# Sevenfold products of a SwiGLU layer in one sequence for every row pair, an earlier place for the first piece of the next matrix, and held-back opening loads

## The chip, the cores and the metric

The kernel runs on one core of a Trainium2 chip (trn2). The metric is device microseconds of one execution. A core has TensorE (PE, matmuls), VectorE (DVE), ScalarE (ACT), GpSimd (POOL) and SyncE (SP); each runs its own instructions in the order of the program, and they wait for one another by semaphores. DMAs are issued here by SP and by POOL.

## The reference

A decoder trunk of two layers on x (1 x 256 x 2048, float32): 256 tokens, width 2048.

```python
def swiglu(x, w_in, w_out):
    g, u = jnp.split(x @ w_in, 2, axis=-1)
    return (jax.nn.silu(g) * u) @ w_out

for layer in range(DEPTH):                      # DEPTH = 2
    hn = rms_norm(h, norm_mix[layer])
    mix = mlstm_mixer(...) if layer % N_MIXERS == 0 else rglru_mixer(...)
    h = h + mix
    h = h + swiglu(rms_norm(h, norm_ffn[layer]), ffn_w_in[layer], ffn_w_out[layer])
return rms_norm(h, norm_final)
```

The change touches only swiglu: w_in is 2048 x 11264 (2 x 5632), w_out 5632 x 2048.

## The kernel before, in words

**Number format.** Every float32 matrix is split into a high part (whi, whix, whit, whio: casts on ACT, L266 and L930) and a low part (wlo, wlox, wlot, wloo: subtractions on DVE, L267). One product is three matmuls: L829, L830 and L831; in most of them L830 reads the low part of the weights.

**The first matrix** (`inner`, `pairs`). It is worked off in 11 blocks j of 512 columns of gate and of 512 of up, each block in 8 row pairs p of 256 rows. A "plain" pair (p=0 always, more in block 0) is eight products into four PSUM banks P2, Q5, Q3 and P4. The other pairs are done by seven products in Strassen's manner, P1, P2, Q3, Q5, P7, Q6 and P4, in the order of the table PRODUCTS; they add up in seven banks over the pairs of the block. P1, P2 and Q3 read whix and wlox (the loaded rows), the other four read whit and wlot (sums of rows, made on DVE at L310, L313 and L314 and split at L266 and L267). Pair 7, the last, has an order of its own, LAST: P1, Q6, P7, Q5, P2, Q3, P4.

**The end of a block.** ds is a buffer with four slices, s0, d0, d1, s1 (`ds`). ACT copies P1 into s0 (L865); DVE makes d0 = Q6 - s0 (L866), d1 = d0 - P7 (L868), adds Q5 to s1 and d0's slices (L871), adds P2 to s0 (L874), Q3 to d0 (L876), takes d1 from P4 (L877); ACT applies silu to s0 (L875) and to d1 (L878); two products on DVE (L880) finish it. PE then transposes the result (tv, L889), and ACT casts it (hh, L543).

**The second matrix** (`outs`, `piece`). The block's 512 rows of w_out are done in 8 pieces: quarters q = 0..3 of the columns by b = 0, 1 (token halves), twelve matmuls each, named out with j, q and b: out420 is block 4, q=2, b=0. Block j's pieces q=0 and 1 are placed in pairs 4 to 7 of block j+1, q=2 and 3 in pairs 0 to 3 of block j+2. The function `between` places them: it is called after every product with left = minus the number of products still to come in the pair, and puts the next piece at left = -2 (even pairs) or -3 (odd pairs). A piece opens by an ACT copy of the sum so far into its bank (L949) and ends by an ACT copy back (L960).

**The load of the second matrix.** Per quarter there are two halves of 256 rows. Half i=0: SP loads rawo, ACT casts whio (L266), DVE subtracts (L267). Half i=1: POOL loads rawo (L923); ACT writes wloo = -rawo (L928); POOL issues a DMA that adds the same weights onto wloo (L929); ACT casts whio (L930). What then stands in wloo is the low part, made without DVE. These names carry j, q and i: wloo421 is block 4, q=2, i=1. It is read by the last six of a piece's twelve matmuls, first by the eighth.

**The order.** Each engine's order is fixed when the program is built, by a scheduler with priorities (`tc.high_priority`), so an edit in one place can move instructions of other engines. "Opening" means block 0 of a layer, where the normalised activations (c_f, L474; p_f) are still being made, raw0_5 is the load of pair 5, and the first two rawo loads of w_out are issued ahead of need.

Of the kernel before, what the change touches and what calls it, by code (L numbers as in the profile page):

```python
# [11 lines left out]
ALU = mybir.AluOpType  # L12
# [23 lines left out]
    ("P1", "A11", "B11"), ("P2", "A12", "B21"), ("Q3", "A3", "B22"),  # L36
    ("Q5", "A5", "T1"), ("P7", "A7", "T3"), ("Q6", "A6", "T2"), ("P4", "A22", "T4"),
)

LAST = tuple(sorted(PRODUCTS, key=lambda c: ("P1", "Q6", "P7", "Q5", "P2", "Q3", "P4").index(c[0])))  # L40
SEVEN = ("A12", "A22", "A11", "A5", "A7", "A6", "A3")


# [1 line left out]
def kernel(  # L45
# [21 lines left out]
    nc = tc.nc  # L67
# [209 lines left out]
    def stream4(w, c0, nk):  # L277

        wv = w.rearrange("(k p) n -> p k n", p=P)
        for kg in range(0, nk, 4):  # L280
# [5 lines left out]
            for i in range(4):  # L286
                yield kg + i, *both[i]

    def is_plain(j, p):
        return p not in SEVENS or j == 0 and p in BOTH  # L290

    def pairs(w, j, held):

        wv = w.rearrange("(k p) n -> p k n", p=P)
        for p in range(NK // 2):
            raw = four("raw", f"{j}_{p}", F32, 3)
            if held and j == 0 and p == 0:

                nc.vector.tensor_copy(raw[0:1, 0, 0:1], h[0:1, NT - 1, 2 * NB - 1:2 * NB])
            for i, c0 in enumerate((j * NB, FF + j * NB)):  # L300
                nc.sync.dma_start(raw[:, 2 * i:2 * i + 2, :], wv[:, 2 * p:2 * p + 2, c0:c0 + NB])
            if is_plain(j, p):
                with tc.high_priority(offset=AHEAD):
                    both = halves(f"{j}_{p}", raw)
                yield p, both
                continue

            with tc.high_priority(offset=AHEAD):
                t = four("sum", f"{j}_{p}", F32, 1)
                nc.vector.tensor_tensor(  # L310
                    t[:, 0:2, :], raw[:, 1:3, :], raw[:, 3:4, :].broadcast_to([P, 2, NB]), op=ALU.add
                )
                nc.vector.tensor_tensor(t[:, 2, :], t[:, 0, :], raw[:, 2, :], op=ALU.add)  # L313
                nc.vector.tensor_tensor(t[:, 3, :], t[:, 2, :], raw[:, 0, :], op=ALU.add)  # L314
                both = halves(f"x{j}_{p}", raw, 3) + halves(f"t{j}_{p}", t, step=2)
            yield p, dict(zip(("B21", "B11", "B22", "T1", "T3", "T2", "T4"), both))
# [489 lines left out]
    NP = NK // 2  # L806

    def ffn(layer, n, nxt):
# [24 lines left out]
        def inner(j, between):  # L833

            ps = {}

            def add(c, a, b, stop):
                first = c not in ps
                if first:
                    ps[c] = bank(c, f"{c}_{j}")  # L840
                product(ps[c], a, b, first, stop)


            ds = fp.tile([P, 4, NB], F32, tag="ds", name=f"ds{j}")
            d0, d1, s0, s1 = (ds[:, i, :] for i in range(4))
            last = max(p for p in SEVENS if not is_plain(j, p))
            for p, ops in pairs(w, j, layer == 1):
                if is_plain(j, p):

                    work = [  # L850
                        (c, n.plain(p, f)[a], ops[2 * side + f], p == NP - 1 and f == 1)
                        for c, side, a in (("Q5", 1, 1), ("P2", 0, 0), ("Q3", 1, 2), ("P4", 0, 1)) for f in range(2)
                    ]
                else:
                    seven = n.seven(p)
                    work = [
                        (c, seven[a], ops[b], p == (last if c in ("P7", "P1", "Q6") else NP - 1))
                        for c, a, b in (LAST if p == NP - 1 else PRODUCTS)
                    ]
                for i, job in enumerate(work):  # L860
                    add(*job)
                    between(j, p, i + 1 - len(work))
                if p == last:
                    with tc.high_priority(offset=AHEAD):
                        nc.scalar.copy(s0, ps["P1"])  # L865
                        nc.vector.tensor_tensor(d0, ps["Q6"], s0, op=ALU.subtract)  # L866

                        nc.vector.tensor_tensor(d1, d0, ps["P7"], op=ALU.subtract)  # L868
            with tc.high_priority(offset=AHEAD):

                nc.vector.tensor_tensor(  # L871
                    ds[:, 0:4:3, :], ps["Q5"].unsqueeze(1).broadcast_to([P, 2, NB]), ds[:, 0:2, :], op=ALU.add
                )
                nc.vector.tensor_tensor(s0, ps["P2"], s0, op=ALU.add)  # L874
                nc.scalar.activation(s0, s0, AF.Silu, scale=n.rstd[:, 0:1])  # L875
                nc.vector.tensor_tensor(d0, ps["Q3"], d0, op=ALU.add)  # L876
                nc.vector.tensor_tensor(d1, ps["P4"], d1, op=ALU.subtract)  # L877
                nc.scalar.activation(d1, d1, AF.Silu, scale=n.rstd[:, 1:2])  # L878
                for b, (u, g) in enumerate(((d0, s0), (s1, d1))):
                    nc.vector.scalar_tensor_tensor(  # L880
                        out=u, in0=u, scalar=n.rstd[:, b:b + 1], in1=g, op0=ALU.mult, op1=ALU.mult
                    )
            return d0, s1
# [13 lines left out]
        def outs(j, hi, lo):  # L897

            wv = ffn_w_out[layer][j * NB:(j + 1) * NB, :].rearrange("(k p) n -> p k n", p=P)
            held = {}

            def load(q, last):
                held.clear() if not last else None
                tiles = held[q] = []
                if last:
                    raw = four("raw", f"o{j}{q}", F32, 2)
                    for i in (0, 2):  # L910
                        nc.sync.dma_start(raw[:, i:i + 2, :], wv[:, i:i + 2, q * NB:(q + 1) * NB])
                    with tc.high_priority(offset=AHEAD):
                        tiles.extend(halves(f"o{j}{q}", raw))
                    return
                for i in range(2):

                    spare = "1" if i and q % 2 else ""
                    raw, wh, wl = (
                        pool_of(f"{what}o{at}").tile([P, 2, NB], dt, tag=f"{what}{i}", name=f"{what}o{j}{q}{i}")
                        for what, dt, at in (("raw", F32, ""), ("whi", F32R, ""), ("wlo", F32R, spare))  # L920
                    )
                    src = wv[:, 2 * i:2 * i + 2, q * NB:(q + 1) * NB]
                    (nc.gpsimd if i else nc.sync).dma_start(raw, src)  # L923
                    with tc.high_priority(offset=AHEAD):
                        if i:

                            with after(*copies[-2:-1]):
                                nc.scalar.activation(wl, raw, AF.Copy, scale=-1.0)  # L928
                            nc.gpsimd.dma_start(wl, src, accum_op=ALU.add)  # L929
                            nc.scalar.copy(wh, raw)  # L930
                        else:
                            split(wh, wl, raw)
                    tiles.extend((wh[:, k, :], wl[:, k, :]) for k in range(2))

            def piece(q, b, last=False):
                if b == 0:
                    load(q, last)
                tiles = held[q]
                bs = slice(b * P, (b + 1) * P)
                hs = h[:, b, q * NB:(q + 1) * NB]  # L940
                name = f"out{j}{q}{b}"
                o = acc(name) if last else pool_of("out").tile([P, NB], F32, tag="out", name=name)


                ends = q == 3 and last and nxt.lag and j == NJ - 1
                first = False if ends else last or fresh.pop() if last or fresh else False
                if not first:
                    with tc.high_priority(offset=AHEAD):
                        nc.scalar.copy(o, hs)  # L949
                for k in range(4):  # L950
                    product(o, (hi[:, k, bs], lo[:, k, bs]), tiles[k], first and k == 0, k == 3, skip_group_check=True)
                if ends:

                    nxt.store(b, o)
                    return
                with tc.high_priority(offset=AHEAD):
                    if first:
                        nc.vector.tensor_tensor(hs, o, hs, op=ALU.add)
                    else:
                        copies.append(nc.scalar.copy(hs, o))  # L960

            return [(piece, q, b) for q in range(4) for b in range(NT)]

        work, turns, late = [], [], []

        def between(j, p, left):

            if left == -2 - p % 2 and work:
                piece, *at = work.pop(0)
                piece(*at)  # L970
            if left == 0 and p == 0:
# [258 lines left out]
```

## Time and profile before

| | us |
|---|---|
| median of 3 runs | 2096.39 (2095.75 to 2098.28) |
| the profiled execution | 2094.86 |
| its span in the trace | 2093.1 |
| mean granted PE clock | 0.998 |
| the two swiglu stretches | about 397 to 1083 and 1390 to 2093 |

The profile lists, by engine, when each instruction started and how long it took; busy shares add these up. In a timeline a row reads: start in us, duration in us, engine, line, operation, output and inputs, and in brackets the time that the engine had been idle and what ended it. Matmuls are pipelined: a row of 0.39 us is followed by the next 0.23 us later. A row with x8 is eight instructions in one.

### The profile page before, as it was taken

How to read it: one execution, taken by the hardware profiler on the slowest of the kernel's cores; microseconds unless marked ns; L12 is line 12 of the kernel's file. 1: busy time of each engine (PE TensorE's matmuls, PEld its weight loads, DVE VectorE, ACT ScalarE, POOL GpSimd, SP SyncE). 2: the span in 40 equal slices, each digit the busy share in tenths (PEclk: the TensorE clock that was granted, in tenths of full speed). 3: DMA queues.
4: the chain of work that ended last, by engine and by line, in shares of the span. 5: the costliest groups of instructions: out<-in, count | busy, mean ns of one | idle time of the engine just before them, and what ended most of it. 6: DMA issues, size and time to landing. Idle time of an engine off the chain costs nothing.

```text
span 2093.1 us, 27909 instructions
## 1 busy us (share of the span) xinstructions
PE 2068.5 (99%) x10424; PEld 1738.0 (83%) x10424; DVE 1746.0 (83%) x1930; ACT 1429.0 (68%) x1739; POOL 195.9 (9%) x218
## 2 busy tenths in 40 slices
PE   9999999999999999999999999999999999999998
PEld 8988888877888888888879999887788888888886
DVE  6655556699999999999976787669999999999995
ACT  5444455567777777877864778556787777887775
POOL 0011110000111111111100000000011111111112
PEclk9999999999999999999999999999999999999999
DMA  7556667656878878888765666665787888888784
GB/s 229 170 162 180 181 177 225 187 178 202 254 223 251 234 223 250 241 237 237 224 197 155 191 190 187 219 214 175 218 243 231 242 232 240 242 228 245 231 238 153
DMA packets 223135, 446.66 MB, mean 213 GB/s; under 512 B 16328, under 2 KB 17048, under 8 KB 222872
## 3 DMA queue, kind: packets, MB, share of 16 engines
q1 hardware_dynamic: 189832, 362.02, 53.5%
q0 software_dynamic: 32448, 81.80, 18.1%
q8 instruction: 81, 1.33, 0.3%
q10 hardware_dynamic: 720, 1.07, 0.1%
q14 instruction: 54, 0.44, 0.1%
HBM read 442.74 MB, written 2.10 MB: 213 GB/s over the span
## 4 chain that ended last, share of the span: by engine, by line
PE 73%; DVE 11%; issue 6%; ACT 4%; DMA 4%; POOL 1%; SPq 0%; ACTq 0%; POOLq 0%; DVEq 0%
PE out L829 5%; PE out L830 5%; PE out L831 5%; PE P L830 5%; PE P L831 5%; PE P L829 5%; PE Q L829 4%; PE Q L830 4%; PE Q L831 4%; DMA rawo<-in_ffn_w_out_dram 3%; DVE wlot L267 2%; DVE wlox L267 2%; PE po L328 2%; PE po L327 2%; PE po L326 2%
## 5 line engine op out<-in xcount | busy, mean ns | idle before, releaser
L266 ACT CAST whit<-sum 128x1024 fp32r<-128x1024 f32 x288 | 301.3, 1050 | 182.4 <-DVE sum L310 144.2
L242 DVE TENSOR_TENSOR wlo<-raw,whi 128x1024 fp32r<-128x1024 f32 (+1 forms) x226 | 273.5, 1213 | 172.3 <-ACT whi L241 169.8
L267 DVE TENSOR_TENSOR wlot<-sum,whit 128x1024 fp32r<-128x1024 f32 x288 | 348.9, 1221 | 36.0 <-ACT whit L266 34.6
L241 ACT CAST whi<-raw 128x1024 fp32r<-128x1024 f32 (+1 forms) x226 | 234.5, 1042 | 193.6 <-PE po L328 40.4
L829 PE MATMUL out<-whio,hh 128*128 128x512 f32 x704 | 275.5, 392 | 1.0 <-ACT hh L543 0.5
L830 PE MATMUL out<-wloo,hh 128*128 128x512 f32 x704 | 273.9, 390 | 0.0
L831 PE MATMUL out<-whio,hh 128*128 128x512 f32 x704 | 273.6, 390 | 0.0
L267 DVE TENSOR_TENSOR wlox<-raw,whix 128x1536 fp32r<-128x1536 f32 x144 | 252.5, 1753 | 23.4 <-ACT whix L266 23.0
L266 ACT CAST whix<-raw 128x1536 fp32r<-128x1536 f32 x144 | 213.6, 1483 | 25.4 <-PE P L831 24.2
L310 DVE TENSOR_TENSOR sum<-raw 128x1024 f32<-128x1024 f32 x144 | 176.2, 1223 | 3.9
L929 POOL DMA_DIRECT2D wloo<-in_ffn_w_out_dram x78 | 94.0, 1205 | 702.9 <-ACT wloo L928 678.2
L829 PEld LDWEIGHTS out<-whio,hh 128*128 128x128 f32 x704 | 132.2, 188 | 30.7 <-ACT out L949 1.7
L830 PEld LDWEIGHTS out<-wloo,hh 128*128 128x128 f32 x704 | 132.2, 188 | 28.2 <-DVE wloo L267 0.7
L831 PEld LDWEIGHTS out<-whio,hh 128*128 128x128 f32 x704 | 132.1, 188 | 27.8
L960 ACT COPY h<-out 128x512 f32<-128x512 f32 x154 | 89.8, 583 | 65.3 <-PE out L831 65.2
L923 POOL DMA_DIRECT2D rawo<-in_ffn_w_out_dram x78 | 59.1, 758 | 755.3 <-ACT whio L930 362.6
L267 DVE TENSOR_TENSOR wloo<-rawo,whio 128x1024 fp32r<-128x1024 f32 (+1 forms) x88 | 117.9, 1339 | 4.4 <-ACT whio L266 4.4
L829 PE MATMUL Q<-whit,p_f 128*128 128x512 f32 x288 | 113.9, 400 | 5.2 <-ACT whit L266 4.5
L830 PE MATMUL P<-wlox,p_f 128*128 128x512 f32 x288 | 113.3, 393 | 4.0 <-DVE wlox L267 3.8
L829 PE MATMUL P<-whix,p_f 128*128 128x512 f32 x288 | 112.3, 398 | 2.7 <-ACT whix L266 2.7
L830 PE MATMUL P<-wlot,p_f 128*128 128x512 f32 x288 | 112.6, 391 | 1.7 <-DVE wlot L267 1.7
L830 PE MATMUL Q<-wlot,p_f 128*128 128x512 f32 x288 | 113.2, 397 | 0.1
(296 smaller groups left out, 5240.9 us busy)
## 6 DMA issues: line engine op xcount, KB each, us to landing
raw<-in_ffn_w_in_dram SPq DMA_DIRECT2D x352, 512.0 KB, 4.8
rawo<-in_ffn_w_out_dram SPq DMA_DIRECT2D x98, 512.0 KB, 6.0
raw<-in_m_w_in_dram SPq DMA_DIRECT2D x94, 512.0 KB, 3.8
rawo<-in_ffn_w_out_dram POOLq DMA_DIRECT2D x78, 512.0 KB, 5.9
wloo<-in_ffn_w_out_dram POOLq DMA_DIRECT2D x78, 512.0 KB, 6.4
raw<-in_r_w_in_dram SPq DMA_DIRECT2D x64, 512.0 KB, 3.9
raw<-in_m_w_out_dram SPq DMA_DIRECT2D x32, 512.0 KB, 3.7
raw<-in_r_w_out_dram SPq DMA_DIRECT2D x32, 512.0 KB, 4.2
```

Of the source, the lines that this page charges most:

```text
L241: nc.scalar.copy(hi[:, i:i + step, 0:ncols], r)
L242: nc.vector.tensor_tensor(lo[:, i:i + step, 0:ncols], r, hi[:, i:i + step, 0:ncols].bitcast(F32), op=ALU.subtract)
L266: nc.scalar.copy(hi, src)
L267: nc.vector.tensor_tensor(lo, src, hi.bitcast(F32), op=ALU.subtract)
L310: nc.vector.tensor_tensor(t[:, 0:2, :], raw[:, 1:3, :], raw[:, 3:4, :].broadcast_to([P, 2, NB]), op=ALU.add)
L326: nc.tensor.matmul(o, lhsT=ah[:, bs], rhs=hi, start=(k == 0), stop=False)
L829: nc.tensor.matmul(o, lhsT=a[0], rhs=b[0], start=start, stop=False, **kw)
L830: nc.tensor.matmul(o, lhsT=a[0], rhs=b[1], start=False, stop=False, **kw)
L831: nc.tensor.matmul(o, lhsT=a[1], rhs=b[0], start=False, stop=stop, **kw)
L923: (nc.gpsimd if i else nc.sync).dma_start(raw, src)
L929: nc.gpsimd.dma_start(wl, src, accum_op=ALU.add)
L960: copies.append(nc.scalar.copy(hs, o))
```

## The change

It has five parts.

1. LAST is gone: pair 7 takes the order of PRODUCTS like all others.
2. A plain pair's products come in the order P2, Q5, Q3, P4 instead of Q5, P2, Q3, P4.
3. Where the last sevenfold pair is p=7 (blocks 1 to 10), P1 is copied by ACT twice, into s0 and into d0 (one more ACT copy per block); P2 is added to s0 early, ahead of Q6; Q6 is taken with d0.
4. In pair 0 `between` puts the piece at left = -6, after the two P2 products, instead of at -2, after six.
5. In block 0, for q=0, the two rawo buffers are first written, one element each, by a POOL copy from raw0_5 (`seen`), so that the loads into them can't start before raw0_5 has landed.

```diff
-LAST = tuple(sorted(PRODUCTS, key=lambda c: ("P1", "Q6", "P7", "Q5", "P2", "Q3", "P4").index(c[0])))
...
+    seen = []
...
+            if j == 0 and p == 5:
+                seen.append(raw)
...
-                        for c, side, a in (("Q5", 1, 1), ("P2", 0, 0), ("Q3", 1, 2), ("P4", 0, 1)) for f in range(2)
+                        for c, side, a in (("P2", 0, 0), ("Q5", 1, 1), ("Q3", 1, 2), ("P4", 0, 1)) for f in range(2)
...
-                        for c, a, b in (LAST if p == NP - 1 else PRODUCTS)
+                        for c, a, b in PRODUCTS
...
                         nc.scalar.copy(s0, ps["P1"])
-                        nc.vector.tensor_tensor(d0, ps["Q6"], s0, op=ALU.subtract)
+                        first = s0
+                        if p == NP - 1:
+                            first = d0
+                            nc.scalar.copy(d0, ps["P1"])
+                            nc.vector.tensor_tensor(s0, ps["P2"], s0, op=ALU.add)
+                        nc.vector.tensor_tensor(d0, ps["Q6"], first, op=ALU.subtract)
...
-                nc.vector.tensor_tensor(s0, ps["P2"], s0, op=ALU.add)
+                if last < NP - 1:
+                    nc.vector.tensor_tensor(s0, ps["P2"], s0, op=ALU.add)
...
+                    if j == 0 and q == 0:
+                        nc.gpsimd.tensor_copy(raw[0:1, 0, 0:1], seen[-1][0:1, 0, 0:1])
                     (nc.gpsimd if i else nc.sync).dma_start(raw, src)
...
-            if left == -2 - p % 2 and work:
+            if left == (-2 - p % 2 if p else -6) and work:
```

In the changed kernel line numbers shift: L829 to L831 become L831 to L833, L865 becomes L867 (and L872 is the new copy), L875 and L878 become L884 and L887, L923, L928, L929 and L930 become L935, L940, L941 and L942, L949 and L960 become L961 and L972, L266 becomes L264, L889 becomes L898, L543 becomes L545.

What the scheduler makes of it, at three places of layer 1. First PE at the start of block 6, before, from the third row of Q3 of pair 0 to the first matmul that reads wloo421 (names: bank, block; weights, block and pair; activation):

```order
8621 L830 MATMUL Q3_6_15340<-wlo6_0_15323,p0_f1_11986 128x512
8622 L831 MATMUL Q3_6_15340<-whi6_0_15322,p0_f1_11986 128x512
8623 L829 MATMUL Q3_6_15340<-whi6_0_15322,p0_f1_11986 128x512
8624 L830 MATMUL Q3_6_15340<-wlo6_0_15323,p0_f1_11986 128x512
8625 L831 MATMUL Q3_6_15340<-whi6_0_15322,p0_f1_11986 128x512
8626 L830 MATMUL out420_15360<-wloo420_15349,hh4_14814 128x512
8627 L831 MATMUL out420_15360<-whio420_15348,hh4_14814 128x512
8628 L829 MATMUL out420_15360<-whio420_15348,hh4_14814 128x512
8629 L830 MATMUL out420_15360<-wloo420_15349,hh4_14814 128x512
8630 L831 MATMUL out420_15360<-whio420_15348,hh4_14814 128x512
8631 L829 MATMUL out420_15360<-whio421_15354,hh4_14814 128x512
8632 L830 MATMUL out420_15360<-wloo421_15355,hh4_14814 128x512
```

The same piece in the changed kernel, from the third row of P2 of pair 0:

```order
8630 L833 MATMUL P2_6_15345<-whi6_0_15341,p0_f1_11998 128x512
8631 L831 MATMUL P2_6_15345<-whi6_0_15341,p0_f1_11998 128x512
8632 L832 MATMUL P2_6_15345<-wlo6_0_15342,p0_f1_11998 128x512
8633 L833 MATMUL P2_6_15345<-whi6_0_15341,p0_f1_11998 128x512
8634 L831 MATMUL out420_15365<-whio420_15353,hh4_14832 128x512
8635 L832 MATMUL out420_15365<-wloo420_15354,hh4_14832 128x512
8636 L833 MATMUL out420_15365<-whio420_15353,hh4_14832 128x512
8637 L831 MATMUL out420_15365<-whio420_15353,hh4_14832 128x512
8638 L832 MATMUL out420_15365<-wloo420_15354,hh4_14832 128x512
8639 L833 MATMUL out420_15365<-whio420_15353,hh4_14832 128x512
8640 L831 MATMUL out420_15365<-whio421_15359,hh4_14832 128x512
8641 L832 MATMUL out420_15365<-wloo421_15360,hh4_14832 128x512
```

The piece out420 moved from behind P2, Q5 and Q3 of pair 0 to behind P2; Q5, Q3 and P4 now follow it. In pair 7 ahead of it stand P1, P2, Q3 and Q5, the piece out411, then P7, Q6 and P4 (before: P1, P7, Q6 and Q5, then out411, then P2, Q3 and P4).

Second ACT at the same boundary, before: from the copy of P1 to the silu of s0.

```order
1299 L865 COPY ds5_14815<-P1_5_14910 128x512
1300 L266 CAST whi6_0_15322<-raw6_0_15319 128x2048
1301 L928 ACTIVATE wloo421_15355<-rawo421_15353 128x1024
1302 L266 CAST whio420_15348<-rawo420_15347 128x1024
1303 L960 COPY h_73<-out411_15282 128x512
1304 L930 CAST whio421_15354<-rawo421_15353 128x1024
1305 L949 COPY out420_15360<-h_73 128x512
1306 L875 ACTIVATE ds5_14815<-ds5_14815,rstd_f1_12669 128x512
```

In the changed kernel, from the copies of P1 to the copy into out420:

```order
1302 L867 COPY ds5_14833<-P1_5_14928 128x512
1303 L872 COPY ds5_14833<-P1_5_14928 128x512
1304 L264 CAST whi6_0_15341<-raw6_0_15338 128x2048
1305 L884 ACTIVATE ds5_14833<-ds5_14833,rstd_f1_12681 128x512
1306 L264 CAST whio420_15353<-rawo420_15352 128x1024
1307 L940 ACTIVATE wloo421_15360<-rawo421_15358 128x1024
1308 L972 COPY h_73<-out411_15300 128x512
1309 L942 CAST whio421_15359<-rawo421_15358 128x1024
1310 L961 COPY out420_15365<-h_73 128x512
```

The L928 that writes wloo421 (now L940) stood directly behind whi6_0; between them stand now the silu and the cast whio420, and ahead of whi6_0 there is one copy more. It is so at pair 7 of blocks 3, 5, 7 and 9 in both layers, and at that of block 2 the L960 copy stands ahead of it too. At pair 7 of blocks 4, 6 and 8 the L928 of q=2 keeps its place between the two casts of whit of pair 7.

Third ACT in the boundary after that, block 6 to block 7, before: the silu of d1 among the casts of pair 1. The last row writes wloo531.

```order
1362 L266 CAST whix7_1_15906<-raw7_1_15899 128x1536
1363 L266 CAST whit7_1_15910<-sum7_1_15902 128x1024
1364 L878 ACTIVATE ds6_15318<-ds6_15318,rstd_f1_12669 128x512
1365 L266 CAST whit7_1_15910<-sum7_1_15902 128x1024
1366 L960 COPY h_73<-out520_15863 128x512
1367 L928 ACTIVATE wloo531_15995<-rawo531_15993 128x1024
```

In the changed kernel:

```order
1366 L264 CAST whix7_1_15926<-raw7_1_15919 128x1536
1367 L264 CAST whit7_1_15930<-sum7_1_15922 128x1024 x2
1368 L972 COPY h_73<-out520_15869 128x512
1369 L940 ACTIVATE wloo531_16015<-rawo531_16013 128x1024
1370 L961 COPY out521_15949<-h_73 128x512
1371 L887 ACTIVATE ds6_15337<-ds6_15337,rstd_f1_12681 128x512
```

The silu of d1 (L878, now L887) stood ahead of the L928 that writes wloo531; it now stands behind it and behind the copy into out521. It is so at the end of all blocks from 2 to 9; at that of block 1 it stood behind already.

## The prediction

> **What bounds the kernel now.** I read the page first, then the busy time of a steady stretch, then the list of what TensorE (PE) waits for, then the timelines of PE, ScalarE (ACT) and GpSimd (POOL) around one block boundary, then the landing times of the loads. The page:
>
> ```profile
> span 2093.1 us, 27909 instructions
> PE 2068.5 (99%) x10424; PEld 1738.0 (83%) x10424; DVE 1746.0 (83%) x1930; ACT 1429.0 (68%) x1739; POOL 195.9 (9%) x218
> ```
>
> The same by stretch, here 1500 to 2000 us (columns: us, then busy us and count for PE, weight load, DVE, ACT, POOL; granted clock, DMA share, GB/s), and what PE waited for in the whole run (total, times, longest):
>
> ```profile
> 1500.00:2000.00 500.00, 498.80 (x2223) 409.45 (x2222) 476.19 (x463) 387.73 (x443) 62.44 (x64) 1.00 0.81 237
> PE Q L829 <- ACT whit L266: 4.5, 10, 1.5
> PE P L830 <- DVE wlox L267: 3.8, 2, 2.2
> PE P L829 <- ACT whix L266: 2.7, 2, 1.3
> PE P L830 <- DVE wlot L267: 1.7, 2, 0.8
> ```
>
> PE is idle for 1.2 us in 500: the feed-forward part runs at the speed of its matmuls. So the change, which leaves out no matmul, can win only the few tenths per block that PE still waits, and it can lose any amount by making PE wait for something that is now early. DVE, at 95% of the same stretch, is the second bound, with little room.
>
> Now one boundary, block 5 to block 6 of layer 1. PE (start, duration; the last two rows are the piece out420, its first matmul and the first one that needs the low half of the load wloo421):
>
> ```profile
> 1732.73 0.39 PE L829 MATMUL P<-whix,p_f 128*128 128x512 f32 x1
> ...
> 1735.96 0.40 PE L829 MATMUL out<-whio,hh 128*128 128x512 f32 x1
> ...
> 1738.72 0.39 PE L829 MATMUL P<-whix,p_f 128*128 128x512 f32 x1
> ...
> 1743.48 0.39 PE L829 MATMUL out<-whio,hh 128*128 128x512 f32 x1
> ...
> 1746.42 0.39 PE L830 MATMUL out<-wloo,hh 128*128 128x512 f32 x1
> ```
>
> From 1738.72 to 1743.48 stand 21 matmuls: 0.227 us from one to the next. I count time from 1732.73, the first matmul of pair 7. The twelve matmuls ahead of 1735.96 would take 12 x 0.227 = 2.72; they took 3.23. These 0.5 us are the wait for ACT's whit that the list names, and they are what the new order of products removes: P1, P2, Q3 need whix alone, so whit has 2 us until Q5.
>
> **What the early piece does to the load it reads.** The same boundary on ACT, then on POOL:
>
> ```profile
> 1732.81 1.05 ACT L266 CAST whit<-sum 128x1024 fp32r<-128x1024 f32 x1
> 1733.76 0.58 ACT L949 COPY out<-h 128x512 f32<-128x512 f32 x1
> 1734.28 0.58 ACT L865 COPY ds<-P 128x512 f32<-128x512 f32 x1
> 1734.76 1.91 ACT L266 CAST whi<-raw 128x2048 fp32r<-128x2048 f32 x1
> 1736.57 1.06 ACT L928 ACTIVATE wloo<-rawo 128x1024 fp32r<-128x1024 f32 x1
> 1737.55 1.05 ACT L266 CAST whio<-rawo 128x1024 fp32r<-128x1024 f32 x1
> ...
> 1740.92 0.73 ACT L875 ACTIVATE ds<-ds,rstd_f 128x512 f32<-128x512 f32 x1
> ```
>
> ```profile
> 1737.93 1.20 POOL L929 DMA_DIRECT2D wloo<-in_ffn_w_out_dram  x1 [11.69 <-ACT wloo L928]
> 1740.80 0.75 POOL L923 DMA_DIRECT2D rawo<-in_ffn_w_out_dram  x1 [1.67 <-ACT whio L930]
> ```
>
> wloo is made in two steps: ACT writes minus the weights (L928), then POOL issues a DMA that adds the weights onto it. How long such an accumulating load takes from issue to landing (min, median, max), of 37 in the blocks of layer 0 and 37 of layer 1:
>
> ```profile
> DMA to landing us min/median/max: 6.0/6.4/8.4
> DMA to landing us min/median/max: 6.0/6.4/9.5
> ```
>
> At this boundary the landing is 1737.93 + 6.4 = 1744.3, or 11.6, and PE wants it at 1746.42, or 13.7: two microseconds early, and so free.
>
> In the changed order both ends move against each other.
>
> Later: ahead of L928 now stand whit, the copy into out, the copy of P1, a second copy of P1, whi, the silu and whio. By the starts above, the second copy costs 0.5 (1734.28 to 1734.76), the silu 0.6 (0.73 less the overlap of neighbours), whio 1.0: L928 starts at 1736.57 + 2.1 = 1738.7 and ends at 1739.75, or 7.0; POOL issues 0.3 later, at 7.3 (before, 1737.63 to 1737.93); landing at 7.3 + 6.4 = 13.7.
>
> Earlier: PE comes to out420 after 12 matmuls of pair 7, the piece out411 (12), the other 9, and only 6 of pair 0: 39 x 0.227 = 8.85. The low half of wloo421 is needed by the eighth matmul of the piece: 8.85 + 7 x 0.227 = 10.4, say 10.5 with ACT's copy into out.
>
> PE idles 13.7 - 10.5 = 3.2 us. Less the 0.5 that went and 0.1 of small waits, that is +2.6 per block. Nothing hides it: the piece stands in one run of twelve, and matmuls of the pair behind it on the same queue can't pass. This holds where L928 stands after whi_0 now: pair 7 of blocks 3, 5, 7 and 9, and of block 2, where one more ACT copy lies in front (0.8 more). In two layers that is ten blocks: 10 x 2.6 + 2 x 0.8 = 27.6.
>
> The bounds: landing in 6.0 gives 2.2 per block. On the other side, the load is now issued at 1740.1, when DMA queues are fuller. The ordinary load that POOL issued at 1740.80 took this long (last column):
>
> ```profile
> rawo<-in_ffn_w_out_dram POOLq DMA_DIRECT2D x1, 512.0 KB, 8.6
> ```
>
> With 8.6 the idle time would be 5.4, and +4.8 per block. I keep the median of the same kind of load.
>
> **The silu behind the next load.** In blocks 4, 6 and 8 L928 for q=2 keeps its early place, but the second silu (L878), formerly ahead of the L928 of q=3, now stands behind it. Here it is in before, block 6: first ACT, then POOL, the landing of that load, and DVE's last product and PE.
>
> ```profile
> 1801.75 1.05 ACT L930 CAST whio<-rawo 128x1024 fp32r<-128x1024 f32 x1
> ...
> 1807.28 0.72 ACT L878 ACTIVATE ds<-ds,rstd_f 128x512 f32<-128x512 f32 x1 [1.02 <-DVE ds L877]
> ...
> 1810.64 1.06 ACT L928 ACTIVATE wloo<-rawo 128x1024 fp32r<-128x1024 f32 x1
> ```
> ```profile
> 1803.10 0.75 POOL L923 DMA_DIRECT2D rawo<-in_ffn_w_out_dram  x1 [6.44 <-ACT whio L930]
> ```
> ```profile
> rawo<-in_ffn_w_out_dram POOLq DMA_DIRECT2D x1, 512.0 KB, 7.5
> ```
> ```profile
> 1808.42 0.74 DVE L880 SCALAR_TENSOR_TENSOR ds<-ds,rstd_f 128x512 f32<-128x512 f32 x1
> ```
> ```profile
> 1794.69 0.39 PE L829 MATMUL P<-whix,p_f 128*128 128x512 f32 x1
> ...
> 1811.22 1.03 PE L889 MATMUL tv<-ident,ds 128*128 128x128 f32 x8
> ```
>
> Counted from 1794.69: the load is issued at 8.4 and lands at 15.9; then L928 (1.0), the copy (0.5), the silu (0.7), DVE's product (0.74) and a handover put the transposes tv at 19.0. PE reaches them after 72 matmuls, 16.3: 2.7 idle. In before tv came at 16.53 after 69 matmuls (15.66), 0.9 late. So +1.8 in each of six blocks: +10.8. Bounds: +1.0 if the load is issued 0.8 earlier, since its cast waits less for PE, +2.3 if the casts ahead of it, one copy longer, delay it by 0.5. In the ten other blocks the same wait falls mostly into the time that PE has already lost: at most 0.7 more.
>
> **What an idle PE does to its clock.** Rows after two of the present idle times, and the granted clock (ahead of the last two columns) behind the first:
>
> ```profile
> 433.20 0.50 PE L830 MATMUL P<-wlox,p_f 128*128 128x512 f32 x1 [2.19 <-DVE wlox L267]
> ...
> 1425.25 0.50 PE L830 MATMUL P<-wlox,p_f 128*128 128x512 f32 x1 [1.57 <-DVE wlox L267]
> ```
> ```profile
> 435.00:438.00 3.00, 3.00 (x8) 2.32 (x7) 2.95 (x3) 1.90 (x1) 0.00 (x0) 0.50 1.02 380
> ```
>
> After 2.19 idle, three microseconds ran at half speed, 1.5 lost; after 1.57 I find none. An idle time of 3.2 lies beyond the first. So each of the ten blocks pays between 0.7 (no slow clock, but the silu's wait shows) and 1.5 (slow clock, which covers it): I take 1.2, 12 in all. The six idle times of 2.7 I take without, with 1.5 each as the bound: 0 to +9.
>
> The Trainium skill ("TensorE: Matmul & The Clock Gate", Part 1) has the clock halved after at least one idle window of about 3.4 us and warns of gaps above that. By it 3.2 us would bring no slow clock and the 12 would shrink to 7; the row of 2.19 speaks against so late a threshold.
>
> **The rest.** At the end of layer 0 this wait goes:
>
> ```profile
> 1055.88 0.74 PE L829 MATMUL Q<-whit,p_f 128*128 128x512 f32 x2 [1.54 <-ACT whit L266]
> ```
>
> P1, P2 and Q3 now cover 1.4 of it: -1.5 with small change; bounds -2 and 0. The opening of each layer: ACT now waits so,
>
> ```profile
> 418.38 1.06 ACT L928 ACTIVATE wloo<-rawo 128x1024 fp32r<-128x1024 f32 x1 [8.73 <-DMA rawo<-in_ffn_w_out_dram]
> ...
> 423.64 0.84 ACT L474 ACTIVATE c_f<-tr_f,cols 128x256 f32<-128x256 f32 x2 [1.99 <-DVE p_f L267]
> ```
> ```profile
> rawo<-in_ffn_w_out_dram POOLq DMA_DIRECT2D x78, 512.0 KB, 5.9
> ```
>
> with whix_5 queued behind. Held back until raw0_5 is there, the two loads come one after the other on POOL: from 409.6 (418.38 - 8.73) 5.9, two casts, 5.9 and one cast, and the c_f behind them on ACT starts at about 424.5 instead of 423.6: +1 for both layers. whix_5, now ahead of the second load, gives DVE a start some 3 us earlier; if that carries to PE, the two waits of 2.19 and 1.57 and the slow clock go, -5. Bounds -5 and +5 (the two loads each 2 us slower). The 1-element POOL copies and the plain pairs' new order are taken at nothing: POOL is 9% busy, and pair 0's matmuls are the same.
>
> **The sum**, against the profiled execution's 2094.86 (the median of the runs shown is 1.5 more): 27.6 + 10.8 + 12 - 1.5 + 1 = 49.9, so 2144.8. I say 2145.
>
> **The rivals.** (1) *The loads land in time*, on the other side. If the accumulating load took 3.2 us from its issue, it would be there at 10.5 just as PE wants it, and an ordinary load as short would free the silu; then only gains stay: 16 boundaries at -0.5, -1.5 and +1, 2086, down to 2080 with the opening. The point that decides is 3.2 against the 6.0 that is the shortest of 74 loads. The Trainium skill ("DMA: Bandwidth & Descriptors", "Anatomy of one DMA — SWDGE (gpsimd) path") fits 2.0 us plus bytes over 436e3 per us, an estimate of 3.2 for these 512 KB; the trace has twice that beside its other traffic. With the chance that ACT runs its row far earlier than I place it: 0.15. (2) *The wait only changes its name*: ACT finds time, the load just makes it, but DVE, at 95%, comes one operation late for Q5 of pair 0 or for tv (0.5 to 0.7, by the 0.74 of its row above less the overlap) in place of the 0.5 removed: 16 x (0 to +0.2), 2094 to 2098. For it speaks how full DVE is; against it that the load is three microseconds off: 0.10. (3) *Worse loads*: landing in 8.6 and slow clocks throughout, 10 x 4.8 + 1.6 + 15 + 10.8 + 9 - 0.5 = 83.9, 2179; part of the forecast's side, 0.10. (4) The forecast, with one of its two waits smaller than I think, 2115 to 2165: 0.65. That the change does not do what it says is out: the order of the instructions has it.
>
> **The numbers.** Slower by over 0.2% (about 4 us, what a measurement here can tell from no change): 0.65 + 0.10 = 0.75. Within: 0.10. Faster: 0.15. The range reaches from 2094, which leaves out rival 1, to 2165, which leaves out half of rival 3. The forecast's own range is 2124 (landing in 6.0, no slow clock, +1.0 in the even blocks, the lower bounds of the rest: 22 + 1.6 + 7 + 6 - 2 - 5 = 29.6) to 2165.
>
> **What would show it.** Right: the waits list of the changed kernel names out (L830 of before) waiting for a DMA of wloo, about ten times at 3 us; tv waiting for DVE about 2 to 3 us in six blocks; the wait for whit gone; PEclk below 1.00 in slices of the two feed-forward parts. Wrong: no matmul waits for wloo, or L928 starts by 5 and its load lands by 10.5; then rival 1 holds. If out waits, but for whio or the copy into out, the place is right and the cause is not.

## The result and the profile after

| | us |
|---|---|
| changed kernel, median of 5 runs | 2201.45 (2199.66 to 2203.08) |
| kernel before, 5 runs beside it | 2096.39 (2094.90 to 2098.97) |
| ratio | 1.0499, 95% interval 1.0484 to 1.0515 |
| the changed kernel's profiled execution | 2203.08, span 2201.3 |

The change costs 105 us. The forecast had the sign, the place and the mechanism, and half of the size: 2145, with a range that ended at 2165. The ratios in this document leave out four single executions of 5358 to 7383 us (one of g_early_wloo, three of the kernel before).

The page of the changed kernel, and what PE waited for (total, times, longest):

```profile
span 2201.3 us, 27893 instructions
PE 2099.6 (95%) x10424; PEld 1754.4 (80%) x10424; DVE 1746.6 (79%) x1930; ACT 1436.1 (65%) x1759; POOL 201.3 (9%) x222
```
```profile
PE out L832 <- DMA wloo<-in_ffn_w_out_dram: 61.7, 10, 6.4
PE out L831 <- ACT out L961: 5.5, 10, 1.6
PE P L832 <- DVE wlox L265: 4.6, 2, 3.5
PE tv L898 <- DVE ds L889: 4.5, 4, 1.6
PE Q L831 <- ACT whit L264: 3.7, 3, 3.3
```

The first row is new and is most of the story: ten waits of 6.2 us for the accumulating load, at the ten places the prediction named. PE's share fell from 99% to 95%. The wait for whit at the boundaries is gone, as forecast; of the 3.7 us in the last row, 3.3 are one wait at the opening of layer 1.

The boundary of block 5 to 6, which the prediction worked out, starts here at 1812.30, the first PE row below. ACT, POOL, SP's issues and PE around it:

```profile
1816.69 0.73 ACT L884 ACTIVATE ds<-ds,rstd_f 128x512 f32<-128x512 f32 x1
1817.31 1.05 ACT L264 CAST whio<-rawo 128x1024 fp32r<-128x1024 f32 x1
1818.26 1.06 ACT L940 ACTIVATE wloo<-rawo 128x1024 fp32r<-128x1024 f32 x1
```
```profile
1819.62 1.21 POOL L941 DMA_DIRECT2D wloo<-in_ffn_w_out_dram  x1 [13.73 <-ACT wloo L940]
```
```profile
1819.44 0.37 SPq L303 DMA_DIRECT2D raw<-in_ffn_w_in_dram  x1
1820.58 0.37 SPq L935 DMA_DIRECT2D rawo<-in_ffn_w_out_dram  x1
1820.99 0.47 SPq L303 DMA_DIRECT2D raw<-in_ffn_w_in_dram  x1
```
```profile
1812.30 0.39 PE L831 MATMUL P<-whix,p_f 128*128 128x512 f32 x1
...
1822.77 0.39 PE L831 MATMUL out<-whio,hh 128*128 128x512 f32 x1
1829.05 0.79 PE L832 MATMUL out<-wloo,hh 128*128 128x512 f32 x1 [5.89 <-DMA wloo<-in_ffn_w_out_dram]
1829.64 0.63 PE L833 MATMUL out<-whio,hh 128*128 128x512 f32 x1
1830.07 0.63 PE L831 MATMUL out<-whio,hh 128*128 128x512 f32 x1
```

ACT writes wloo behind the silu and whio, as forecast; POOL issues the load at 7.3 by the prediction's clock, as forecast. But the load is there only 9.4 us later:

```profile
wloo<-in_ffn_w_out_dram POOLq DMA_DIRECT2D x1, 512.0 KB, 9.4
```

And after the wait PE runs slow: its rows start 0.43 us apart (1829.64, 1830.07) instead of 0.227. The granted clock of that stretch (the column ahead of the last two):

```profile
1829.00:1832.00 3.00, 2.95 (x7) 2.37 (x8) 0.00 (x0) 0.36 (x1) 0.00 (x0) 0.50 1.04 396
```

### The profile page after: what moved, and what is told of

The parts are those of the page before. It is cut to its first block, busy times and chain, and to the rows that moved or that the text cites. A ratio compares the mean times of both kernels' runs of the same rounds, so it can differ in the third digit from the quotient of the medians.

```text
span 2201.3 us, 27893 instructions
## 1 busy us (share of the span) xinstructions
PE 2099.6 (95%) x10424; PEld 1754.4 (80%) x10424; DVE 1746.6 (79%) x1930; ACT 1436.1 (65%) x1759; POOL 201.3 (9%) x222
## 4 chain that ended last, share of the span: by engine, by line
issue 52%; PE 36%; POOL 7%; DMA 2%; DVE 1%; ACT 1%; POOLq 0%; SPq 0%; ACTq 0%
POOL wloo L941 4%; PE po L328 2%; PE po L330 2%; PE po L329 2%; POOL rawo L935 2%; DMA rawo<-in_ffn_w_out_dram 2%; PE qk L347 1%; PE qk L345 1%; PE qk L346 1%; PE o L330 1%; PE v L328 1%; PE v L329 1%; PE rec L345 1%; PE o L329 1%; PE v L330 1%
## 5 line engine op out<-in xcount | busy, mean ns | idle before, releaser
L264 ACT CAST whit<-sum 128x1024 fp32r<-128x1024 f32 x288 | 299.7, 1051 | 141.1 <-DVE sum L312 125.0
L832 PE MATMUL out<-wloo,hh 128*128 128x512 f32 x704 | 282.0, 401 | 62.1 <-DMA wloo<-in_ffn_w_out_dram 61.7
L831 PE MATMUL out<-whio,hh 128*128 128x512 f32 x704 | 279.4, 397 | 6.2 <-ACT out L961 5.5
L833 PE MATMUL out<-whio,hh 128*128 128x512 f32 x704 | 278.7, 397 | 0.0
L264 ACT CAST whix<-raw 128x1536 fp32r<-128x1536 f32 x144 | 213.4, 1482 | 63.7 <-PE P L833 63.7
L972 ACT COPY h<-out 128x512 f32<-128x512 f32 x154 | 90.0, 584 | 138.7 <-PE out L833 138.5
L831 PEld LDWEIGHTS out<-whio,hh 128*128 128x128 f32 x704 | 133.6, 190 | 42.1 <-ACT out L961 13.3
L941 POOL DMA_DIRECT2D wloo<-in_ffn_w_out_dram x78 | 94.3, 1208 | 762.5 <-ACT wloo L940 747.1
L833 PEld LDWEIGHTS out<-whio,hh 128*128 128x128 f32 x704 | 135.1, 192 | 27.7 <-DVE hh L546 0.2
L940 ACT ACTIVATE wloo<-rawo 128x1024 fp32r<-128x1024 f32 x78 | 82.9, 1062 | 57.1 <-DMA rawo<-in_ffn_w_out_dram 56.9
L831 PE MATMUL Q<-whit,p_f 128*128 128x512 f32 x288 | 113.7, 395 | 3.7 <-ACT whit L264 3.7
L831 PE MATMUL P<-whix,p_f 128*128 128x512 f32 x288 | 113.5, 402 | 2.7 <-ACT whix L264 2.7
L264 ACT CAST whio<-rawo 128x1024 fp32r<-128x1024 f32 (+1 forms) x88 | 101.1, 1149 | 21.6 <-PE out L833 17.4
```

The costliest lines, as they stand in the source:

```text
L264: nc.scalar.copy(hi, src)
L831: nc.tensor.matmul(o, lhsT=a[0], rhs=b[0], start=start, stop=False, **kw)
L832: nc.tensor.matmul(o, lhsT=a[0], rhs=b[1], start=False, stop=False, **kw)
L833: nc.tensor.matmul(o, lhsT=a[1], rhs=b[0], start=False, stop=stop, **kw)
```

## The experiments

Theory 1: the new order of products makes ACT write wloo 2 us later; the load is thereby issued at the very moment at which SP starts its own loads, and takes 9.6 (the median of the ten) instead of 6.3; both together make PE wait 6.2 and lose its clock. Rivals: the early place of the piece by itself (part 4); the sheer number of loads then under way, or POOL's own next load; and, for the remainder, the hold-back (part 5).

| run | what it is | median us | ratio to before (95%) |
|---|---|---|---|
| a_place_back | changed, part 4 undone | 2198.96 | 1.0496 (1.0481 to 1.0512) |
| b_no_hold | changed, part 5 undone | 2187.67 | 1.0439 (1.0414 to 1.0464) |
| f_shift_raw | changed, half a raw load held | 2196.23 | 1.0493 (1.0475 to 1.0510) |
| g_early_wloo | changed, wloo written early | 2127.73 | 1.0153 (1.0136 to 1.0170) |
| f2_shift_both | changed, raw load held | 2180.85 | 1.0405 (1.0389 to 1.0421) |
| f3_rawo_on_sp | changed, a POOL load on SP | 2193.83 | 1.0467 (1.0453 to 1.0481) |
| d_hold_only | before, part 5 alone | 2107.10 | 1.0049 (1.0036 to 1.0061) |
| k_q3_second | before, another order of the last pair | 2103.54 | 1.0035 (1.0022 to 1.0048) |
| f4_shift_three | changed, raw and rawo held | 2161.62 | 1.0312 (1.0297 to 1.0328) |
| m_early_no_hold | g without part 5 | 2115.80 | 1.0096 (1.0081 to 1.0111) |
| c_place_only | before, part 4 alone | 2101.43 | 1.0027 (1.0017 to 1.0036) |
| h_dve_low | changed, no such load for q=2 | 2127.22 | 1.0151 (1.0136 to 1.0166) |

**Is it the place of the piece?** Part 4 undone:

```diff
-            if left == (-2 - p % 2 if p else -6) and work:
+            if left == -2 - p % 2 and work:
```

> Part 4 undone: the piece of pair 0 is asked for after six products again. In the order of the instructions ten of its twelve matmuls stand at the same place all the same, ahead of Q5, since Q5's bank comes free later; the load wloo and its ACT row (L940) stand where they stand in the changed kernel. Theory 1 (the accumulating load is issued late, by the new ACT order, and beside SP's loads): nothing gained, 2195 to 2205. Rival (the early place of the piece is what makes PE wait): 2105 to 2115.

Nothing gained. PE's waits:

```profile
PE out L832 <- DMA wloo<-in_ffn_w_out_dram: 61.8, 10, 6.4
```

The same ten waits. But this edit does not move the piece back: as its expectation says, ten of the twelve matmuls stay ahead of Q5 all the same. And part 4 alone, on the kernel before (the same diff read backwards):

> The kernel before with part 4 alone, the piece after the two P2 products of pair 0. Pair 7 keeps its old order, and ACT writes wloo early, between the casts of whit. If it is the order of the products, not the piece, that makes the load late: 2094 to 2101. If the early piece by itself makes PE wait for wloo: over 2115.

It cost 5.7 us (a ratio of 1.0027), no more. (In that kernel the first two products of pair 0 are Q5's, not P2's as the expectation has it.) POOL issued the load early there, and no PE row waits for it. So the diff's most visible line, taken out or put in, is nearly innocent. The place of the piece is not tested by these two: in the first it stayed early, and in the second only its first part moved up, while its first matmul that reads wloo421 came about half a microsecond earlier than before (block 5 to 6 of layer 1). An estimate from the rows: issued at 7.3 and landing 9.4 later, the load is there at 16.7, so the old place of the piece, with its need at 13.7, would have made the wait shorter by some 3 us and not removed it. What makes the load late is ACT's new order. It comes with parts 1 to 3; which of them brings it is not shown, since no run takes these three apart.

**Is it ACT's order?** One row moved: the write of wloo gets a higher priority for q=2, and stands between the casts of whit in pair 7, ahead of the copies of P1 and earlier than in the kernel before, where it stood behind P1's copy at these boundaries.

```diff
-                            with after(*copies[-2:-1]):
+                            with after(*copies[-2:-1]), tc.high_priority(offset=1000 if q == 2 else 0):
                                 nc.scalar.activation(wl, raw, AF.Copy, scale=-1.0)
```

> The changed kernel with one ACT row moved: the write of wloo for q=2 gets a higher priority and stands between the two casts of whit of pair 7 in all blocks, ahead of the copies of P1. Theory 1 (issue late by ACT's order): the load is issued at 1 instead of 7.5 us after the start of pair 7 and lands by 8.5 to 10.5, PE needs it at 10.5: the ten waits of 6.2 and their slow clocks go, 2201 - 95 = 2106 (2100 to 2112; the opening's +10 stays). Rival (the place of the piece, or DVE late at Q5 and tv, is the bound): PE waits 1 us or more for DVE instead at each boundary, 2120 to 2150.

No PE row waits for wloo's DMA any more, and 74 us are gone. PE's longest lists now:

```profile
PE P L832 <- DVE wlox L265: 6.8, 2, 3.4
PE tv L898 <- DVE ds L889: 4.4, 4, 1.8
PE P L832 <- DVE wlo L265: 3.8, 9, 1.4
PE out L831 <- ACT out L961: 3.4, 6, 2.0
```

The theory's number was missed by some 20: 2127.7 lies within the 2120 to 2150 of the rival. Small waits for DVE and ACT stand where the wait for whit stood. So the rival that "the wait changes its name" is true as well, beside theory 1. Taking the load away altogether gives the same time:

```diff
-                        if i:
+                        if i and q != 2:
                             with after(*copies[-2:-1]):
```

> The changed kernel with the low half for q=2 made by a DVE subtraction (1.2 us more of DVE per block) in place of the accumulating load. If that load is what PE waits for, the ten waits of 6.2 and their slow clocks go, and DVE's extra work shows in part: 2105 to 2130. If ordinary loads at that place are as late: over 2150.

2127.2, within its bounds, and no PE row waits for wloo's DMA: the ten waits hang on this one load.

**Why 9.6 us?** First try: hold SP's raw load of pair 3, at the five boundaries per layer, by a one-element POOL copy behind the issue of wloo.

```diff
+            if p == 3 and j in (3, 4, 6, 8, 10):
+                add, rawo = adds[-1]
+                with after(add):
+                    nc.gpsimd.tensor_copy(raw[0:1, 0, 0:1], rawo[0:1, 0, 0:1])
...
-                            nc.gpsimd.dma_start(wl, src, accum_op=ALU.add)
+                            add = nc.gpsimd.dma_start(wl, src, accum_op=ALU.add)
+                            if q == 2:
+                                adds.append((add, raw))
```

> The changed kernel, and at the five boundaries per layer where PE waits for wloo the SP load that started 0.2 us before it (raw of pair 3) is held by a POOL copy of one element until POOL has issued wloo, some 1.4 us later. ACT's and PE's orders are as in the changed kernel. Theory 1 (a wloo load that starts within 0.7 us of two SP loads takes 8 to 10 us, one that starts over 1.2 us ahead of them takes 6.3): wloo takes 6.3 in place of 9.6, PE waits 2.9 instead of 6.2, 2201 - 33 = 2168, down to 2143 if the slow clock goes too. Rival (the load is slow because of the whole traffic of those microseconds or because of POOL's own next load behind it): it takes 9 to 10 as now, 2196 to 2206.

The load took 8.6 to 9.9 and the time moved by nothing that the interval can tell. But the edit had missed its aim: it held one half of the raw load only, and the other still started 0.2 us (at two boundaries 0.65) ahead of wloo. So it decides nothing. The second try holds both halves (shown against the first):

```diff
-                    nc.gpsimd.tensor_copy(raw[0:1, 0, 0:1], rawo[0:1, 0, 0:1])
+                    nc.gpsimd.tensor_copy(raw[0:1, 0:4:2, 0:1], rawo[0:1, 0:2, 0:1])
```

> The changed kernel with both halves of the raw load of pair 3 held by the POOL copy until wloo has been issued (f_shift_raw held only the second one: its first half still started 0.2 us ahead of wloo). Now only SP's rawo starts about 1 us behind wloo, the two raw halves 1.4 us or more, POOL's own rawo 1.9. Theory 1 (who starts first at the DMA engines counts): wloo takes 6.3 to 7, PE waits 2.9 to 3.6 in place of 6.2, time 2201 - 30 = 2171 (2140 if the slow clock goes with it). Rival (whole traffic, or POOL's own next load): 9 to 10 us, 2194 to 2203.

Half way, between theory and rival: PE waits 4.4 instead of 6.2 each time, and the load takes 8.0 at the boundary shown (7.2 to 8.1 over the ten).

```profile
PE out L836 <- DMA wloo<-in_ffn_w_out_dram: 44.1, 10, 4.6
```
```profile
1803.26 1.21 POOL L945 DMA_DIRECT2D wloo<-in_ffn_w_out_dram  x1 [13.74 <-ACT wloo L944]
```
```profile
1804.22 0.37 SPq L939 DMA_DIRECT2D rawo<-in_ffn_w_out_dram  x1
1804.69 1.02 SPq L307 DMA_DIRECT2D raw<-in_ffn_w_in_dram  x2
```

SP's rawo still follows 0.96 us behind. In another run, on the changed kernel, POOL's own next load is moved to SP:

```diff
-                    (nc.gpsimd if i else nc.sync).dma_start(raw, src)
+                    (nc.gpsimd if i and q != 3 else nc.sync).dma_start(raw, src)
```

> The changed kernel with the rawo load of q=3, half 1, issued by SP in place of POOL, so that POOL issues nothing behind wloo. Rival (POOL's own next load, issued 1.4 us later on the same queue, slows wloo): wloo takes 6.3 to 8, time 2160 to 2185. Theory 1 (SP's load that starts just ahead of it): 9 to 10 as before, 2195 to 2206.

The waits stay (60.5 us in ten): that rival falls. (The time is 7 us below the changed kernel's by the ratios and 1 below the theory's bounds; of this, PE's waits for whit went from 3.7 to 0.7.) Last, the run of the second try with rawo held too:

```diff
+                    if q == 3 and i == 0 and j in (1, 2, 4, 6, 8):
+                        add, rawo = adds[-1]
+                        with after(add):
+                            nc.gpsimd.tensor_copy(raw[0:1, 0, 0:1], rawo[0:1, 0, 0:1])
```

> As f2_shift_both, with SP's rawo for q=3 held too (there it started 1.0 us behind wloo, and wloo took 8.0 us in place of 9.6). Now no SP load starts from 0.2 us ahead of wloo to 1.2 us behind it. If the loads that start within a microsecond are the whole of it: wloo takes 6.3 to 6.6, PE waits 2.9 to 3.2, 2181 - 16 = 2165. If what is left comes from the sheer number of loads then under way: 7.5 to 8, 2177 to 2184.

```profile
1790.03 1.21 POOL L949 DMA_DIRECT2D wloo<-in_ffn_w_out_dram  x1 [13.74 <-ACT wloo L948]
```
```profile
1791.31 0.37 SPq L943 DMA_DIRECT2D rawo<-in_ffn_w_out_dram  x1
1791.79 1.77 SPq L307 DMA_DIRECT2D raw<-in_ffn_w_in_dram  x2
```
```profile
wloo<-in_ffn_w_out_dram POOLq DMA_DIRECT2D x1, 512.0 KB, 6.3
```
```profile
PE out L836 <- DMA wloo<-in_ffn_w_out_dram: 27.7, 10, 3.3
```

With SP's first load 1.28 us behind wloo instead of 0.18 ahead of it, wloo takes 6.3 here (5.9 to 6.8 over the ten) and PE waits 2.8. The same five loads of 512 KB are issued within some 2.5 us in both kernels, so their number is not the reason; what differs is whose packets move first. The DMA view counts packets by queue: q1 carries SP's loads, q0 POOL's. In the changed kernel, the first 2.5 us after POOL issued wloo (1819.6 to 1822.1):

```profile
q1 hardware_dynamic: 210, 0.43, 53.9%
```

None of wloo has moved yet, 0.43 MB of SP's have. In f4_shift_three, the first 4.9 us (1790 to 1794.9):

```profile
q0 software_dynamic: 200, 0.41, 51.8%
```

Here POOL's queue has the engines to itself. POOL's first packet moved 1.9 us after its issue (1791.94); SP's first, in the changed kernel, 1.0 us after its own (1820.46). That is why an SP load issued a little behind wloo can still be ahead of it. By the time wloo had landed, 2.07 MB had moved in the changed kernel (9.4 us at 220 GB/s) and 0.75 MB in f4_shift_three (6.3 us at 119). The trace of before had shown it. In block 6 SP issued two raw loads 0.19 us behind the wloo load that POOL issued at 1795.43, and that load took 9.5:

```profile
1795.43 1.22 POOL L929 DMA_DIRECT2D wloo<-in_ffn_w_out_dram  x1 [6.83 <-ACT wloo L928]
```
```profile
1795.62 0.88 SPq L301 DMA_DIRECT2D raw<-in_ffn_w_in_dram  x2
```
```profile
wloo<-in_ffn_w_out_dram POOLq DMA_DIRECT2D x1, 512.0 KB, 9.5
```

In block 5 they came 1.27 us behind the load of 1737.93, and that took 6.3:

```profile
1739.20 0.92 SPq L301 DMA_DIRECT2D raw<-in_ffn_w_in_dram  x2
```
```profile
wloo<-in_ffn_w_out_dram POOLq DMA_DIRECT2D x1, 512.0 KB, 6.3
```

**The hold-back.** Part 5's lines are taken out of the changed kernel:

```diff
-                    if j == 0 and q == 0:
-
-                        nc.gpsimd.tensor_copy(raw[0:1, 0, 0:1], seen[-1][0:1, 0, 0:1])
```

> Part 5 undone: the opening loads aren't held back. The changed kernel reaches the end of block 0 4.9 us later than before in layer 0 and 5.3 us later in layer 1. If the hold-back is the cause: 2201 - 10 = 2191 (2188 to 2194), with the ten waits for wloo as they were. If the new order of the plain pairs is the cause: 2199 to 2203.

The same lines, and those that fill `seen`, alone in the kernel before:

> The kernel before with part 5 alone, the held-back opening loads. b_no_hold took 14 us off the changed kernel. If the hold-back costs by itself: 2096 + 10 = 2106 (2102 to 2110), the end of block 0 about 5 us later in each layer. If it costs only together with the new order of the plain pairs: 2094 to 2099.

It costs 10.3 alone (0.0049 of 2096; 7.5 to 12.8 by the interval) and 12.6 in company (1.0499 less 1.0439; the four times of b_no_hold spread over 12.7 us, so this is known to a few microseconds only). The ten waits for wloo stay without it. ACT at the opening of layer 0 in the changed kernel:

```profile
416.88 1.06 ACT L940 ACTIVATE wloo<-rawo 128x1024 fp32r<-128x1024 f32 x1 [8.73 <-DMA rawo<-in_ffn_w_out_dram]
...
425.58 1.06 ACT L940 ACTIVATE wloo<-rawo 128x1024 fp32r<-128x1024 f32 x1 [4.49 <-DMA rawo<-in_ffn_w_out_dram]
426.55 0.82 ACT L476 ACTIVATE c_f<-tr_f,cols 128x256 f32<-128x256 f32 x2
```

In the kernel before, the 8.73 of the prediction's row was the wait for the second load, and ACT had not waited for the first. Now ACT waits as long for the first load and then 4.49 for the second, with c_f behind: 426.55 against 423.64 before. In d_hold_only the longest wait of PE for wlox grows from 2.2 to 3.5 us.

**Do the parts add up, and is there a better version?** The edit of g_early_wloo, and part 5 taken out:

> g_early_wloo without the held-back opening loads: parts 1 to 4 with wloo issued early. If the parts add up: 2128 - 12 = 2116 (2112 to 2120), still 20 over the kernel before, from the small waits of PE for DVE and ACT (tv, the copy into out, wlo, wloo) that the new order brings in place of the wait for whit. If the hold-back only costs together with the late load: 2124 to 2130.

They do: 2115.8. In ratios, of 0.0499: 0.0187 for SP's loads beside wloo (changed less f4), 0.0159 for the late issue by itself with the slow clocks behind it (f4 less g, where the issue is earlier than in the kernel before), 0.0057 for the hold-back (g less m), 0.0096 left in m for the order's small waits, of which part 4 alone makes 0.0027. In microseconds 39, 33, 12 and 20, together 105. None of these beats the kernel before. A gentler order of the last pair on it, meant to give whit its time:

```diff
-LAST = tuple(sorted(PRODUCTS, key=lambda c: ("P1", "Q6", "P7", "Q5", "P2", "Q3", "P4").index(c[0])))
+LAST = tuple(sorted(PRODUCTS, key=lambda c: ("P1", "Q3", "Q6", "P7", "Q5", "P2", "P4").index(c[0])))
```

> The kernel before with one edit: the last pair's order is P1, Q3, Q6, P7, Q5, P2, P4 instead of P1, Q6, P7, Q5, P2, Q3, P4, so that whit has one more product's time (0.68 us) before PE needs it, and Q6 and P7 stay early. If the waits for whit (about 0.5 us at 16 boundaries and 1.5 at the end of layer 0) just go: 2096 - 9 = 2087. If DVE or ACT turn up in their place, as after g_early_wloo: 2093 to 2100.

Slower by 7, outside both expectations. The waits for whit went from 4.5 to 0.8 us, but PE's listed waits came to 1 us more in all, and PE was busy 4.6 us longer (2073.1 against 2068.5) with the same 10424 matmuls; what stretched them stays open.

## Why the prediction was right and wrong

**The mechanism was right.** The order of ACT's rows delays the issue to 7.3, the piece needs the load three microseconds earlier (10.7 instead of 13.7, by 1822.77 and 1812.30), PE waits at the eighth matmul of the first piece of pair 0, at ten boundaries, and matmuls at half speed follow each of the ten waits. f4_shift_three comes nearest to the prediction as it was drawn: loads of 5.9 to 6.8, a wait of 2.8 (3.2 forecast), and six of the ten waits followed by matmuls 0.43 us apart. It measures 2162; that this lies only 17 above 2145 hides two terms below that were some 10 too small each.

**The step that failed** is "I keep the median of the same kind of load": landing after 6.4. It was 9.4 to 9.9 in every one of the ten. The same two rows of the prediction held the maximum of 9.5, and the rows behind them would have told that the long ones are those that start beside SP's loads: of the 74 loads, 24 took over 7.5 us, and each of these had an SP load that started within 0.7 us of it. I asked how long such a load takes, and not what starts beside it at its new place, though the prediction noted that queues are fuller there; its upper bound of 8.6 was a load of another kind. The ten waits were 32 us (3.2 each) and became 62.

**The clock** was mis-sized with it: 1.5 us lost was the upper bound and 1.2 was taken, 12 in all. Behind the waits of 6.2 PE ran five to thirteen matmuls at 0.43 each time, and lost 1.5 to 3.0 us, 24 in all. After the waits of f4 it was seven to eleven matmuls in six places (1.7 to 2.7 us) and none in four, so the 12 would have been right for the load as it was drawn, as an average over two cases that the prediction did not tell apart. One of the six:

```profile
1796.40 0.50 PE L836 MATMUL out<-wloo,hh 128*128 128x512 f32 x1 [2.80 <-DMA wloo<-in_ffn_w_out_dram]
...
1798.23 0.63 PE L836 MATMUL Q<-wlo,p_f 128*128 128x512 f32 x1
1798.65 0.63 PE L837 MATMUL Q<-whi,p_f 128*128 128x512 f32 x1
```

In f4 a wait of 2.66 us had the slow clock behind it, and waits of 2.67 and 2.90 had not. The Trainium skill ("TensorE: Matmul & The Clock Gate", Part 1) says that the window in which activity is counted runs free of the program; that nearly the same wait has the slow clock at one boundary and not at the next agrees with it. Its figure of about 3.4 us for an idle window does not fit here as a threshold: 2.80 us (f4) and 2.19 (before) were enough.

**The hold-back** was +1, bounds -5 and +5, and is +10 to +13: c_f starts 2.9 us later in layer 0 instead of the forecast 0.9, and the wait for wlox grew instead of going. That the one makes the other is argued from the order of the rows and not shown by a run. The one-element POOL copies, taken at nothing, took 0.9 to 2.2 us each at the two openings.

**The silu behind the next load** was +10.8. tv waits 4.5 us in all, at four of the six places named: right place, less than half the size.

**Rival 2**, waits that only change their names, I gave 0 to +3 and took for an alternative. It came on top: m_early_no_hold keeps 20 us without any wait for wloo. Its list of PE's waits shows part of it,

```profile
PE tv L898 <- DVE ds L889: 5.4, 5, 2.4
PE P L832 <- DVE wlox L265: 4.3, 2, 2.4
PE out L831 <- ACT out L958: 4.0, 6, 2.5
```

but these rows don't add up to 20 over before. In the profiles PE's listed waits come to 9 us more than before (25.0 against 15.8), and PE is busy 11 us longer (2079.8 against 2068.5) with the same 10424 matmuls; what stretched these stays open.

**Rival 1**, the load in time, needed a landing in 3.2 us. The shortest that any of these traces shows is 5.8. The Trainium skill's estimate of 3.2 ("DMA: Bandwidth & Descriptors", "Anatomy of one DMA — SWDGE (gpsimd) path"), which the prediction gave beside it, is little more than half of that.

**In sum.** By the ratios, the late issue with its slow clocks made 33 us where the forecast had 40 (27.6 and 12), the hold-back 12 where it had 1, the small waits 20 where it had 9 (10.8 less 1.5). These would make some 2161. The other 39 are SP's loads beside wloo, which the forecast left out by keeping the median (its rival 3, with 8.6, had a part of them).

## What to carry to other kernels

When an edit changes the order of one engine's work, follow every DMA whose issue depends on that engine, and ask both when it is issued now and which other loads start within a microsecond of it; a median over all loads of its kind hides two groups. Undo the parts of a change one by one before believing the visible line: here the line that asks for the piece early cost 6 us alone, while the new order of products with its second copy of P1, which was to remove half a microsecond per block, cost most of 105 through a row that it pushed back on another engine. A wait of 3 us on PE can cost more than 3 us: in f4 the slow clock behind six of ten such waits took another 1.7 to 2.7.

## What the runs showed of the hardware

In the traces of all runs, an accumulating load of 512 KB issued by POOL took 5.9 to 6.8 us where SP's first load started 1.2 to 3 us behind it (95 loads, none of SP's starting in the 2 us ahead), 7.1 to 8.1 where that was 0.9 to 1.2 us (21), and 7.6 to 9.9 where the first started between 0.8 us ahead of it and 0.9 behind (255). The shortest of all was 5.8, with no SP load starting near it.

A PE wait of 3.0 us or more inside the feed-forward parts always had matmuls at 0.43 us behind it; of those of 1.9 to 2.9 us, some had and some had not.

A POOL copy of one element lasted between 0.2 us (f4) and, at the openings of the changed kernel, 0.9 to 2.2 us:

```profile
408.90 0.88 POOL L934 COPY rawo<-raw 1x1 f32<-1x1 f32 x1 [5.82 <-DMA raw<-in_ffn_w_in_dram]
...
438.80 2.08 POOL L934 COPY rawo<-raw 1x1 f32<-1x1 f32 x1 [10.65 <-DVE m_f L265]
```
